# A transformer trunk on one Trainium2 core: turned blocks at fixed tiles, in source order

## The chip, the cores and the metric

The kernel runs on one core of a Trainium2 chip. The core has a matmul engine (TensorE, PE in the profile; its weight loads are PEld), three engines for elementwise work (VectorE or DVE, ScalarE or ACT, GpSimd or POOL), and SyncE (SP), which here only issues DMAs. Each engine works through its own queue of instructions in order; semaphores make one wait for another. The metric is the device time of one execution in microseconds, smaller is better.

## The reference

Two residual layers on 256 tokens of 2048 features, all in float32. Each layer is a token mixer and an MLP, each behind an RMSNorm:

```python
for i in range(DEPTH):                     # DEPTH = 2
    h = rms_norm(x, norm_mix[i])
    x = x + mixer(h, ...)                  # i = 0: stick-breaking attention; i = 1: indexer-selected softmax attention
    h = rms_norm(x, norm_mlp[i])
    x = x + jnp.square(jax.nn.relu(h @ w_up[i])) @ w_down[i]      # d_ff = 8192
```

Mixer A (layer 0) projects to q, k, v (16 heads of 128), weights each earlier token by sigmoid(z) times the product of (1 - sigmoid(z)) of the tokens between, and projects back. Mixer B (layer 1) scores tokens with a small indexer, keeps the best 64 per query, runs grouped softmax attention on them (16 query heads, 4 key heads), and projects back. Nearly all the arithmetic is in the weight matrices: the two MLPs alone have 4 x 2048 x 8192 weights.

## The kernel before, in words

**Weight tiles.** All dense products run as a list of 738 items (class `Item`), each one weight tile of 256 x 512 numbers (128 partitions x 1024). For item i the main loop at the end of `trunk` does, in this order: `split(i + 2)` (L762) makes of a raw weight tile a high part (ScalarE copy in a rounded format, through `copy`, L83) and a low part (VectorE subtraction, L774); `load(i + 7)` (L750) issues the DMA of a later raw tile on SyncE (L756; five raw buffers, so it waits for the split that frees one); the item's own matmuls (L271 to L273: three products, high x high, high x low, low x high, for two token halves and two blocks of 128 rows, twelve in all); then the item's `post` functions; then what is due. The split tiles have three buffers, so a split waits for the matmuls of the item three places earlier.

**Turned blocks.** Eight items (one group of 512 output columns) end in a 256 x 512 result with tokens on the partitions. Where the next product needs features on the partitions, `to_features` (L155) turns the block: VectorE transposes 32 x 32 squares into a tile `y` (L160), SyncE writes `y` to DRAM in four DMAs (`write`, L163 to L167, tile `td`), and reads it back turned (`read`, L169 to L171) into a tile `z`. A function `then` takes it up. `y` and `z` share the name `jx` and three buffers. There are 54 such blocks: 8 of q and k in mixer A, 2 of the indexer's queries in mixer B (these ten have no `then`), 12 of the residual stream x (`turn`, L180: four after each of mixer A, the first MLP, and mixer B), and 32 of the MLPs' hidden layers (`up_done`, L316). `turn` scales the block by a gain and splits it into the high and low parts of `xT`; `up_done` applies relu and square (L319) and splits into `hT` (copy L83, subtraction L322).

**When.** `later(n, f)` (L151) puts f into the list of the item n places on. Before the change a block that ends with item T is written with item T+2, read with T+5, and taken up in two halves with T+7 and T+8.

**Order.** These places are only the order in which the program is traced. The tile framework then schedules each engine's queue by its own model of time (`schedule_with_timeline_sim=True`), and may put an instruction ahead of earlier traced ones if its model says that it is ready sooner. `tc.keep_in_program_order(ins)` forbids that for one instruction: it can't be queued ahead of the one traced just before it on its engine. `pin` does the same for the first 16 items alone. So before the change the writes, the reads and the uptake were free to move, and so are the splits, loads and dense matmuls after item 16, before and after the change.

Groups run one after the other, except at the start of each section and in the output projections, where `side_by_side` (L292) interleaves two or three groups, so that they end close together. Mixer A's steps per pair of heads (`z_step`, `tail_step`, `o_step`) and mixer B's (`score_step` and the rest) hang on fixed items as `post` functions.

Of the kernel before, what the change touches and what calls it, by code (L numbers as in the profile page):

```python
# [9 lines left out]
F32 = mybir.dt.float32  # L10
F32R = mybir.dt.float32r
BF16 = mybir.dt.bfloat16
AF = mybir.ActivationFunctionType
OP = mybir.AluOpType
# [3 lines left out]
P = 128  # L18
# [41 lines left out]
def trunk(ctx, tc, x, x_t, gains_t, w_in_a, w_out_a, w_in_b, w_out_b, rel_bias, w_up, w_down, out):  # L60


    nc = tc.nc
# [10 lines left out]
    act, dve, pool, pe = nc.scalar, nc.vector, nc.gpsimd, nc.tensor  # L74

    pinned = [True]

    def pin(ins):
        if pinned[0]:
            tc.keep_in_program_order(ins)  # L80

    def copy(o, i, scale=1.0):
        pin(act.activation(o, i, AF.Copy, scale=scale))  # L83
# [67 lines left out]
    def later(n, f, *a):  # L151

        due[clock[0] + n].append(lambda: f(*a))

    def to_features(halves, place, then):  # L155


        y = tmp.tile([P, 8, P], F32, name="jx", bufs=3)
        for t, h in enumerate(halves):
            dve.transpose(y[:, 4 * t:4 * t + 4, :].rearrange("p k f -> p (k f)"), h)  # L160
        d = drp.tile([4, 32, 8, 4, 32], F32, name="td", bufs=4)

        def write():  # L163
            for a in range(4):
                nc.sync.dma_start(d[:, :, :, a, :].rearrange("b j n i -> j n b i"),  # L165
                                  y[32 * a:32 * a + 32].rearrange("p n (b i) -> p n b i", b=4))
            later(3, read)  # L167

        def read():  # L169
            z = place()  # L170
            nc.sync.dma_start(z, d.rearrange("b j n a i -> (b j) n (a i)"))  # L171
            if then is not None:
                later(2, then, z)

        later(2, write)

    def any_tile():
        return tmp.tile([P, 8, P], F32, name="jx", bufs=3)

    def turn(c, col):  # L180

        def half(z, js):
            for j in js:
                kt = 4 * c + j
                g = gains[:, col + kt:col + kt + 1]
                zk = z.rearrange("p (t k) q -> p t k q", t=2)[:, :, j, :]
                h, l = (xT[:, kt, i, :].rearrange("p (t q) -> p t q", t=2) for i in range(2))
                copy(h, zk, scale=g)
                dve.scalar_tensor_tensor(l, zk, g, h.bitcast(F32), op0=OP.mult, op1=OP.subtract)

        def split_in(z):
            half(z, (0, 1))
            later(1, half, z, (2, 3))

        to_features([xs[:, t, c * 512:(c + 1) * 512] for t in range(2)], any_tile, split_in)
        for t in range(2):
            square(c, t)

# [34 lines left out]
    def tokens_out(items, key, w, r0, c0, lhs, q, done, apart=False):  # L233


        def first(wh, wl):

            acc = accp.tile([P, 2, 512], F32, name="acc")
            accs[key] = [acc[:, t, :] for t in range(2)]
            L = lhs()  # L240
            for j in range(KB):
                for n, (part, wx) in enumerate(((0, wh), (1, wh), (0, wl))):
                    for t in range(2):
                        pin(pe.matmul(accs[key][t], L[:, j, part, t * P:(t + 1) * P], wx[:, j, :],
                                      start=(j == 0 and n == 0), stop=False))

        def last(acc, L, wh, wl):

            for t, c0, c1 in ((0, 0, 512), (1, 0, 256), (1, 256, 512)):
                for j in range(KB):  # L250
                    k = KB * q + j
                    for n, (part, wx) in enumerate(((0, wh), (0, wl), (1, wh))):
                        tc.keep_in_program_order(pe.matmul(
                            acc[t][:, c0:c1], L[:, k, part, t * P:(t + 1) * P], wx[:, j, c0:c1],
                            start=False, stop=(j, n) == (KB - 1, 2), skip_group_check=c0 > 0))

        def mm(wh, wl):
            if q == 0 and apart:
                accs[key] = [auxp.tile([P, 512], F32, name="aux") for _ in range(2)]
            elif q == 0:  # L260
                acc = accp.tile([P, 2, 512], F32, name="acc")
                accs[key] = [acc[:, t, :] for t in range(2)]
            acc, L = accs[key], lhs()
            if apart and q == QB - 1:
                last(acc, L, wh, wl)
                return
            for t in range(2):
                for j in range(KB):
                    k = KB * q + j
                    ts = slice(t * P, (t + 1) * P)  # L270
                    pin(pe.matmul(acc[t], L[:, k, 0, ts], wh[:, j, :], start=(k == 0), stop=False))  # L271
                    pin(pe.matmul(acc[t], L[:, k, 0, ts], wl[:, j, :], start=False, stop=False))  # L272
                    pin(pe.matmul(acc[t], L[:, k, 1, ts], wh[:, j, :], start=False,  # L273
                                  stop=(k == KT - 1)))
        it = Item(rows(w, r0 + KB * P * q, KB * P, c0, 512), KB, 512,
                  mm if len(items) >= LEAD else first, True)
        if q == QB - 1:
            it.post.append(lambda: done(accs.pop(key)))
        items.append(it)
# [24 lines left out]
    def mlp(l, next_col):  # L304
        items = []
        sec = {}
# [7 lines left out]
            dve.tensor_mul(sec["rs2"], rs, rs)  # L314

        def up_done(f, c, acc):  # L316
            def half(z, t):
                r = z[:, 4 * t:4 * t + 4]
                dve.scalar_tensor_tensor(r, r, 0.0, r, op0=OP.max, op1=OP.mult)  # L319
                h, l = (sec[f][:, 4 * c:4 * c + 4, i, t * P:(t + 1) * P] for i in range(2))  # L320
                copy(h, r)
                dve.tensor_sub(l, r, h.bitcast(F32))  # L322

            def split_in(z):
                if c == 0:
                    sec[f] = sec["pool"].tile([P, KT, 2, S], F32R, name="hT", bufs=2)
                half(z, 0)
                later(1, half, z, 1)

            to_features(acc, any_tile, split_in)  # L330

        def down_done(f, g, acc):
            if f < 3 or next_col is not None:
# [31 lines left out]
    def mixer_a():  # L365
# [102 lines left out]
            items[at].post.append(lambda n=n: square(n // 2, n % 2))  # L468
        items[2 * QB - 2].post.insert(0, stats)
        out_proj(items, w_out_a, lambda: st["oT"], 32, 2)  # L470
        for f, at in ((z_step, (23, 27, 47, 51, 71, 75, 87, 89)),
                      (tail_step, (27, 31, 51, 55, 75, 79, 92, 94)),
                      (o_step, (31, 34, 55, 58, 89, 91, 96, 98))):
            for hp, i in enumerate(at):
                items[i].post.append(lambda f=f, hp=hp: f(hp))
        return items, begin
# [6 lines left out]
    def bias_rows(pl):  # L483

        rb = pl.tile([P, 32], F32, name="rb", bufs=1)
        tc.keep_in_program_order(nc.scalar.dma_start(
            rb, rel_bias.unsqueeze(1).to_broadcast([HEADS, P // HEADS, 32])))
        bv = pl.tile([P, REL], F32, name="bv", bufs=1)  # L490
        for k, (lo, hi) in enumerate(zip(BUCKET_FROM, BUCKET_FROM[1:] + [256])):
            pool.tensor_copy(bv[:, 256 - hi:256 - lo], rb[:, k:k + 1].to_broadcast([P, hi - lo]))
            lo, hi = max(lo, 1), min(hi, 128)
            if lo < hi:
                pool.tensor_copy(bv[:, 255 + lo:255 + hi],
                                 rb[:, 16 + k:17 + k].to_broadcast([P, hi - lo]))
        bias["rows"] = bv

    def bias_spread(n):
        to = bv_d.rearrange("h (r q) d -> (h r) q d", r=P // HEADS)[:, 4 * n:4 * n + 4, :]  # L500
        tc.keep_in_program_order(
            nc.scalar.dma_start(to, bias["rows"].unsqueeze(1).to_broadcast([P, 4, REL])))

    def mixer_b():
# [61 lines left out]
        def score_step(m):  # L566
# [3 lines left out]
            ps = accp.tile([P, 2, 512], F32, name="acc")  # L570
            for t, cs, w in ((0, TOKS[0], P), (1, TOKS[1], S)):
                for i, lo in enumerate(halves):
                    tc.keep_in_program_order(
                        pe.matmul(ps[:, i, cs], st["qiT"][lo, m // 4, 4 * t + m % 4], kiT[lo, 0:w],
                                  start=True, stop=True))
            rl = mk([P, 2, 384], "rl")
# [31 lines left out]

        def bias_mask(n, h):
            b = st["bias", n][:, h:h + 2]  # L610
            tc.keep_in_program_order(
                dve.tensor_tensor(b, b, st["mask"].unsqueeze(1).to_broadcast([P, 2, 384]), op=OP.add))

        def normed(acc, key):
# [101 lines left out]
        def at(i, f, *a):  # L716
            items[i].post.append(lambda: f(*a))

        at(k0 + 1, wi_step)
        for m, d in enumerate((5, 5, 7, 7, 9, 9, 11, 11)):  # L720
            at(k0 + d, score_step, m)
        at(k0 + 9, lambda: turned("k", st["kT"], gains[:, 65:66]))
        at(k0 + 12, admit)
        for r in range(TOPK // 8):
            at(k0 + 13 + r // 2, top_step)
        at(k0 + 17, mask_step)
        for n in range(4):
            j = q0 + QB * n
            at(j, bias_load, n)
# [10 lines left out]
    n = 0  # L740
# [96 lines left out]
```

## Time and profile before

| | us |
|---|---|
| device time, median of 3 runs | 2160.94 (2158.61 to 2162.93) |
| the profiled execution | 2164.39 |
| span in its profile, first to last instruction | 2162.7 |

| engine | busy us | share |
|---|---|---|
| TensorE | 2105.7 | 97% |
| VectorE | 1236.8 | 57% |
| ScalarE | 969.6 | 45% |
| GpSimd | 28.5 | 1% |

The profile has several views. The *page* gives the busy time of each engine; matmuls are pipelined and their ends modelled, so that a matmul counts for longer than the distance to the next. The *waits* say which engine sat idle before which line, and what ended the wait: total us, times, longest. The *timeline* lists instructions by start and duration, with idle time and its cause in brackets. *Windows* give the busy time of a stretch, the clock granted to TensorE (1.00 is full) and the DMA engines' busy share. A *tile's* view gives the instructions that touch one tile, with the shortest, median and longest duration in ns, and its DMAs' times from issue to landing. Line numbers are those of the code above; L83 is the helper `copy`, so the tile's name tells which copy it is.

### The profile page before, as it was taken

The page shows a single profiled execution, that of the slowest core. Times are in us where ns is not written, and L with a number is a line of the kernel's source. Part 1 is how long each engine was busy: PE and PEld are TensorE (multiplying, and loading weights), DVE is VectorE, ACT ScalarE, POOL GpSimd, SP SyncE. Part 2 cuts the span into 40 slices and gives each one's busy share as a digit, 9 for nine tenths or more (in the row PEclk, how much of TensorE's full clock was granted, in tenths as well). Part 3 has the DMA queues.
Part 4 walks back from the last instruction along what each step waited for, and adds up shares of the span by engine and source line. Part 5 has one row for each costly group of instructions (what it writes and reads, how often), then busy time and mean ns, then how long its engine had stood idle before and what let it go on. Part 6 is the DMA issues. An engine that isn't in the chain of part 4 may idle for free.

```text
span 2162.7 us, 24794 instructions
## 1 busy us (share of the span) xinstructions
PE 2105.7 (97%) x9312; PEld 1726.7 (80%) x9312; DVE 1236.8 (57%) x1403; ACT 969.6 (45%) x1207; POOL 28.5 (1%) x71
## 2 busy tenths in 40 slices
PE   9999999999999999999999999999999999998999
PEld 7888887777788778778878788878777887887887
DVE  6555556565554644554565877665554555555554
ACT  6554555444333433433444566554443343344333
POOL 0200000000000000000000000000000000000000
PEclk9999999999999999999999999999999999999999
DMA  8788747788766866776688565598786687687664
GB/s 297 221 235 245 216 160 218 229 243 242 211 198 196 230 191 194 225 206 193 203 240 259 164 181 165 149 256 230 223 231 192 194 229 217 196 220 208 198 204 153
DMA packets 447113, 457.50 MB, mean 212 GB/s; under 512 B 240336, under 2 KB 250640, under 8 KB 446992
## 3 DMA queue, kind: packets, MB, share of 16 engines
q1 hardware_dynamic: 439136, 448.46, 70.9%
q10 hardware_dynamic: 7856, 7.45, 1.1%
q8 instruction: 73, 1.20, 0.2%
q14 instruction: 48, 0.39, 0.1%
HBM read 422.23 MB, written 33.55 MB: 211 GB/s over the span
## 4 chain that ended last, share of the span: by engine, by line
PE 73%; DMA 15%; DVE 5%; SPq 4%; issue 2%; ACT 1%; DVEq 0%; ACTq 0%
PE acc L272 23%; PE acc L273 23%; PE acc L271 22%; DMA jx<-td 6%; DMA td<-jx 6%; DVE w L774 3%; SPq L165 2%; SPq L756 2%; DMA wraw<-in_w_down_dram 2%; ACT w L83 1%; DVE jx L160 1%; DMA wraw<-in_w_up_dram 1%; DVE jx L319 1%; PE aux L660 0%; ACT xT L83 0%
## 5 line engine op out<-in xcount | busy, mean ns | idle before, releaser
L774 DVE TENSOR_TENSOR w<-wraw,w 128x1024 fp32r<-128x1024 f32 (+1 forms) x739 | 897.7, 1219 | 661.8 <-ACT w L83 659.7
L83 ACT ACTIVATE w<-wraw 128x1024 fp32r<-128x1024 f32 (+1 forms) x739 | 779.0, 1060 | 925.5 <-PE acc L273 896.0
L272 PE MATMUL acc<-w,xT 128*128 128x512 f32 x1632 | 641.9, 393 | 24.6 <-DVE w L774 24.6
L271 PE MATMUL acc<-w,xT 128*128 128x512 f32 x1632 | 639.6, 392 | 1.1 <-ACT w L83 0.7
L273 PE MATMUL acc<-w,xT 128*128 128x512 f32 x1632 | 638.3, 391 | 0.0
L272 PE MATMUL acc<-w,hT 128*128 128x512 f32 x992 | 390.2, 393 | 19.7 <-DVE w L774 19.7
L271 PE MATMUL acc<-w,hT 128*128 128x512 f32 x992 | 389.4, 393 | 0.2 <-ACT w L83 0.2
L273 PE MATMUL acc<-w,hT 128*128 128x512 f32 x992 | 389.2, 392 | 0.0
L272 PEld LDWEIGHTS acc<-w,xT 128*128 128x128 f32 x1632 | 307.2, 188 | 96.3 <-DVE w L774 33.7
L271 PEld LDWEIGHTS acc<-w,xT 128*128 128x128 f32 x1632 | 307.3, 188 | 66.8 <-ACT w L83 2.0
L273 PEld LDWEIGHTS acc<-w,xT 128*128 128x128 f32 x1632 | 307.3, 188 | 63.4 <-issue 0.3
L272 PEld LDWEIGHTS acc<-w,hT 128*128 128x128 f32 x992 | 188.1, 190 | 62.2 <-DVE w L774 22.9
L271 PEld LDWEIGHTS acc<-w,hT 128*128 128x128 f32 x992 | 188.0, 190 | 40.2 <-ACT w L83 0.9
L273 PEld LDWEIGHTS acc<-w,hT 128*128 128x128 f32 x992 | 188.3, 190 | 39.0
L319 DVE SCALAR_TENSOR_TENSOR jx<-jx 128x512 f32<-128x512 f32 x64 | 41.4, 689 | 144.4 <-DMA jx<-td 126.8
L272 PE MATMUL acc<-w,oT 128*128 128x512 f32 x256 | 101.1, 395 | 1.4 <-DVE w L774 1.4
L271 PE MATMUL acc<-w,oT 128*128 128x512 f32 x256 | 100.6, 394 | 0.8 <-ACT w L83 0.8
L273 PE MATMUL acc<-w,oT 128*128 128x512 f32 x256 | 100.3, 392 | 0.0
L83 ACT ACTIVATE hT<-jx 128x512 fp32r<-128x512 f32 x64 | 39.5, 631 | 125.0 <-DVE jx L319 125.0
L272 PEld LDWEIGHTS acc<-w,oT 128*128 128x128 f32 x256 | 48.1, 188 | 11.9 <-DVE w L774 2.1
L271 PEld LDWEIGHTS acc<-w,oT 128*128 128x128 f32 x256 | 48.0, 188 | 10.9 <-ACT w L83 1.2
L273 PEld LDWEIGHTS acc<-w,oT 128*128 128x128 f32 x256 | 48.1, 188 | 10.1 <-DVE oT L696 0.4
(143 smaller groups left out, 819.5 us busy)
## 6 DMA issues: line engine op xcount, KB each, us to landing
wraw<-in_w_up_dram SPq DMA_DIRECT2D x256, 512.0 KB, 4.6
wraw<-in_w_down_dram SPq DMA_DIRECT2D x256, 512.0 KB, 4.8
wraw<-in_w_in_a_dram SPq DMA_DIRECT2D x95, 512.0 KB, 4.7
wraw<-in_w_in_b_dram SPq DMA_DIRECT2D x64, 512.0 KB, 4.4
td<-jx SPq DMA_DIRECT2D x216, 128.0 KB, 4.7
jx<-td SPq DMA_DIRECT2D x44, 512.0 KB, 5.6
wraw<-in_w_out_a_dram SPq DMA_DIRECT2D x32, 512.0 KB, 3.7
wraw<-in_w_out_b_dram SPq DMA_DIRECT2D x32, 512.0 KB, 4.0
```

The lines of the kernel that those rows point to most:

```text
L83: pin(act.activation(o, i, AF.Copy, scale=scale))
L160: dve.transpose(y[:, 4 * t:4 * t + 4, :].rearrange("p k f -> p (k f)"), h)
L165: nc.sync.dma_start(d[:, :, :, a, :].rearrange("b j n i -> j n b i"), y[32 * a:32 * a + 32].rearrange("p n (b i) -> p n b i", b=4))
L271: pin(pe.matmul(acc[t], L[:, k, 0, ts], wh[:, j, :], start=(k == 0), stop=False))
L272: pin(pe.matmul(acc[t], L[:, k, 0, ts], wl[:, j, :], start=False, stop=False))
L273: pin(pe.matmul(acc[t], L[:, k, 1, ts], wh[:, j, :], start=False, stop=(k == KT - 1)))
L319: dve.scalar_tensor_tensor(r, r, 0.0, r, op0=OP.max, op1=OP.mult)
L756: pin(nc.sync.dma_start(raws[i][:, a], it.src[:, a]))
L774: pin(dve.tensor_sub(wl[:, a], raw[:, a], wh[:, a].bitcast(F32)))
```

## The change

The write, the read and the uptake of turned blocks are pinned to source order, other places are given to them, and the uptake is one operation to a tile instead of two halves:

- `write` at T+1 instead of T+2, and `read` four items later instead of three, so at T+5 as before; all five DMAs of a block are kept in program order on SyncE.
- `then` four items after the read instead of two, at T+9.
- `turn`: with T+9 four ScalarE copies, with T+10 four VectorE subtractions (before: two of each, in turn, at T+7 and at T+8).
- `up_done`: with T+9 one relu-square over the whole 128 x 1024 block, with T+10 one copy, with T+11 one subtraction (before: all three on each half, at T+7 and at T+8).
- Mixer A's and mixer B's steps that hang on turned data move by one or two items.

```diff
         def write():
             for a in range(4):
-                nc.sync.dma_start(...)
-            later(3, read)
+                keep(nc.sync.dma_start(...))
+            later(4, read)
 
         def read():
             z = place()
-            nc.sync.dma_start(z, d.rearrange("b j n a i -> (b j) n (a i)"))
+            keep(nc.sync.dma_start(z, d.rearrange("b j n a i -> (b j) n (a i)")))
             if then is not None:
-                later(2, then, z)
-
-        later(2, write)
+                later(4, then, z)
+
+        later(1, write)
...
-        def half(z, js):
-            for j in js:
-                kt = 4 * c + j
-                ...
-                copy(h, zk, scale=g)
-                dve.scalar_tensor_tensor(l, zk, g, h.bitcast(F32), op0=OP.mult, op1=OP.subtract)
-
-        def split_in(z):
-            half(z, (0, 1))
-            later(1, half, z, (2, 3))
+        def high(z):
+            for j, g, h, l in views():
+                keep(act.activation(h, z.rearrange("p (t k) q -> p t k q", t=2)[:, :, j, :],
+                                    AF.Copy, scale=g))
+            later(1, low, z)
+
+        def low(z):
+            for j, g, h, l in views():
+                keep(dve.scalar_tensor_tensor(l, ..., g, h.bitcast(F32), op0=OP.mult, op1=OP.subtract))
...
         def up_done(f, c, acc):
-            def half(z, t):
-                r = z[:, 4 * t:4 * t + 4]
-                dve.scalar_tensor_tensor(r, r, 0.0, r, op0=OP.max, op1=OP.mult)
-                ...
-                copy(h, r)
-                dve.tensor_sub(l, r, h.bitcast(F32))
+            def relu2(z):
+                ...
+                keep(dve.scalar_tensor_tensor(z, z, 0.0, z, op0=OP.max, op1=OP.mult))
+                later(1, high, z)
+
+            def high(z):
+                r, h, l = parts(z)
+                keep(act.activation(h, r, AF.Copy))
+                later(1, low, z)
+
+            def low(z):
+                r, h, l = parts(z)
+                keep(dve.tensor_sub(l, r, h.bitcast(F32)))
...
-        for f, at in ((z_step, (23, 27, 47, 51, 71, 75, 87, 89)),
-                      (tail_step, (27, 31, 51, 55, 75, 79, 92, 94)),
-                      (o_step, (31, 34, 55, 58, 89, 91, 96, 98))):
+        for f, at in ((z_step, (25, 28, 49, 52, 73, 76, 89, 91)),
+                      (tail_step, (29, 33, 53, 57, 77, 80, 93, 95)),
+                      (o_step, (33, 36, 57, 60, 89, 91, 97, 99))):
...
-        for m, d in enumerate((5, 5, 7, 7, 9, 9, 11, 11)):
+        for m, d in enumerate((6, 6, 8, 8, 10, 10, 12, 12)):
             at(k0 + d, score_step, m)
```

In mixer B, `admit`, the eight `top_step`s and `mask_step` follow one item later as well. Elsewhere `tc.keep_in_program_order` is only renamed to `keep`.

More of the change, by code (lines that the diff above doesn't have):

```diff
@@ L76, in trunk @@
     pinned = [True]
+    keep = tc.keep_in_program_order
     def pin(ins):
         if pinned[0]:
-            tc.keep_in_program_order(ins)
+            keep(ins)
     def copy(o, i, scale=1.0):
@@ L164, in write @@
             for a in range(4):
-                nc.sync.dma_start(d[:, :, :, a, :].rearrange("b j n i -> j n b i"),
-                                  y[32 * a:32 * a + 32].rearrange("p n (b i) -> p n b i", b=4))
-            later(3, read)
+                keep(nc.sync.dma_start(d[:, :, :, a, :].rearrange("b j n i -> j n b i"),
+                                       y[32 * a:32 * a + 32].rearrange("p n (b i) -> p n b i", b=4)))
+            later(4, read)
         def read():
             z = place()
-            nc.sync.dma_start(z, d.rearrange("b j n a i -> (b j) n (a i)"))
+            keep(nc.sync.dma_start(z, d.rearrange("b j n a i -> (b j) n (a i)")))
             if then is not None:
-                later(2, then, z)
-        later(2, write)
+                later(4, then, z)
+        later(1, write)
     def any_tile():
@@ L180, in turn, with views @@
     def turn(c, col):
-        def half(z, js):
-            for j in js:
+        def views():
+            for j in range(4):
                 kt = 4 * c + j
-                g = gains[:, col + kt:col + kt + 1]
-                zk = z.rearrange("p (t k) q -> p t k q", t=2)[:, :, j, :]
                 h, l = (xT[:, kt, i, :].rearrange("p (t q) -> p t q", t=2) for i in range(2))
-                copy(h, zk, scale=g)
-                dve.scalar_tensor_tensor(l, zk, g, h.bitcast(F32), op0=OP.mult, op1=OP.subtract)
-        def split_in(z):
-            half(z, (0, 1))
-            later(1, half, z, (2, 3))
-        to_features([xs[:, t, c * 512:(c + 1) * 512] for t in range(2)], any_tile, split_in)
+                yield j, gains[:, col + kt:col + kt + 1], h, l
+        def high(z):
[5 more added lines that the diff above has]
+            for j, g, h, l in views():
+                keep(dve.scalar_tensor_tensor(
+                    l, z.rearrange("p (t k) q -> p t k q", t=2)[:, :, j, :], g, h.bitcast(F32),
+                    op0=OP.mult, op1=OP.subtract))
+        to_features([xs[:, t, c * 512:(c + 1) * 512] for t in range(2)], any_tile, high)
         for t in range(2):
@@ L252, in last @@
                     for n, (part, wx) in enumerate(((0, wh), (0, wl), (1, wh))):
-                        tc.keep_in_program_order(pe.matmul(
+                        keep(pe.matmul(
                             acc[t][:, c0:c1], L[:, k, part, t * P:(t + 1) * P], wx[:, j, c0:c1],
@@ L316, in up_done, with parts @@
         def up_done(f, c, acc):
-            def half(z, t):
-                r = z[:, 4 * t:4 * t + 4]
-                dve.scalar_tensor_tensor(r, r, 0.0, r, op0=OP.max, op1=OP.mult)
-                h, l = (sec[f][:, 4 * c:4 * c + 4, i, t * P:(t + 1) * P] for i in range(2))
-                copy(h, r)
-                dve.tensor_sub(l, r, h.bitcast(F32))
-            def split_in(z):
+            def parts(z):
+                hT = sec[f][:, 4 * c:4 * c + 4].rearrange("p k i (t q) -> p i t k q", t=2)
+                return z.rearrange("p (t k) q -> p t k q", t=2), hT[:, 0], hT[:, 1]
+            def relu2(z):
                 if c == 0:
                     sec[f] = sec["pool"].tile([P, KT, 2, S], F32R, name="hT", bufs=2)
-                half(z, 0)
-                later(1, half, z, 1)
-            to_features(acc, any_tile, split_in)
+                keep(dve.scalar_tensor_tensor(z, z, 0.0, z, op0=OP.max, op1=OP.mult))
[7 more added lines that the diff above has]
+                keep(dve.tensor_sub(l, r, h.bitcast(F32)))
+            to_features(acc, any_tile, relu2)
         def down_done(f, g, acc):
@@ L487, in bias_rows @@
         rb = pl.tile([P, 32], F32, name="rb", bufs=1)
-        tc.keep_in_program_order(nc.scalar.dma_start(
+        keep(nc.scalar.dma_start(
             rb, rel_bias.unsqueeze(1).to_broadcast([HEADS, P // HEADS, 32])))
@@ L500, in bias_spread @@
         to = bv_d.rearrange("h (r q) d -> (h r) q d", r=P // HEADS)[:, 4 * n:4 * n + 4, :]
-        tc.keep_in_program_order(
+        keep(
             nc.scalar.dma_start(to, bias["rows"].unsqueeze(1).to_broadcast([P, 4, REL])))
@@ L572, in score_step @@
                 for i, lo in enumerate(halves):
-                    tc.keep_in_program_order(
+                    keep(
                         pe.matmul(ps[:, i, cs], st["qiT"][lo, m // 4, 4 * t + m % 4], kiT[lo, 0:w],
@@ L610, in bias_mask @@
             b = st["bias", n][:, h:h + 2]
-            tc.keep_in_program_order(
+            keep(
                 dve.tensor_tensor(b, b, st["mask"].unsqueeze(1).to_broadcast([P, 2, 384]), op=OP.add))
@@ L719, in mixer_b @@
         at(k0 + 1, wi_step)
-        for m, d in enumerate((5, 5, 7, 7, 9, 9, 11, 11)):
+        for m, d in enumerate((6, 6, 8, 8, 10, 10, 12, 12)):
             at(k0 + d, score_step, m)
         at(k0 + 9, lambda: turned("k", st["kT"], gains[:, 65:66]))
-        at(k0 + 12, admit)
+        at(k0 + 13, admit)
         for r in range(TOPK // 8):
-            at(k0 + 13 + r // 2, top_step)
-        at(k0 + 17, mask_step)
+            at(k0 + 14 + r // 2, top_step)
+        at(k0 + 18, mask_step)
         for n in range(4):
```

## The prediction, made before the changed kernel was run

> **What bounds the kernel now.** I read the page first, then the waits of TensorE, cut by stage, then the timeline of one stall on each engine, and last the rows that price the moved operations.
>
> ```profile
> span 2162.7 us, 24794 instructions
> PE 2105.7 (97%) x9312; PEld 1726.7 (80%) x9312; DVE 1236.8 (57%) x1403; ACT 969.6 (45%) x1207; POOL 28.5 (1%) x71
> ```
> TensorE is busy for 97% of the span, and no other engine comes near. So a gain must come out of the 57.0 us in which TensorE is idle (2162.7 - 2105.7), or out of its pace. The next rows are its waits between 340 and 1130 us (mixer A's output projection, first MLP, start of mixer B), then those from 1400 us to the end (mixer B's output projection, second MLP).
>
> ```profile
> PE acc L272 <- DVE w L774: 25.3, 16, 4.7
> PE acc L244 <- ACT w L83: 1.5, 2, 0.8
> PE acc L271 <- ACT w L83: 1.3, 3, 0.8
> ```
> ```profile
> PE acc L272 <- DVE w L774: 20.4, 14, 3.5
> PE acc L244 <- ACT w L83: 1.5, 1, 1.5
> PE acc L271 <- ACT w L83: 0.5, 1, 0.5
> ```
> The columns are total us, times and longest. That is 28.1 + 22.4 = 50.5 us in 37 waits, all for a weight tile not yet split: 45.7 us of it for the low half (VectorE, L774). What keeps VectorE and ScalarE from splitting in time stands in the waits of all engines:
>
> ```profile
>   DVE jx L319: 126.8, 27
>   ACT xT L83: 44.6, 13
> ```
> These are the waits on the turned blocks' tile jx, 40 of them (total us, times). Taken up are 32 up blocks and 12 residual blocks, 44 in all, so nearly each makes its engine wait. One case, on VectorE (start, us, what; idle before and its cause in brackets):
>
> ```profile
> 547.38 1.31 DVE L160 STREAM_TRANSPOSE jx<-acc 128x512 f32<-128x512 f32 x2 [0.40 <-PE acc L273]
> 548.61 1.18 DVE L774 TENSOR_TENSOR w<-wraw,w 128x1024 fp32r<-128x1024 f32 x1
> ...
> 556.63 1.23 DVE L774 TENSOR_TENSOR w<-wraw,w 128x1024 fp32r<-128x1024 f32 x1 [1.49 <-ACT w L83]
> 563.16 1.30 DVE L319 SCALAR_TENSOR_TENSOR jx<-jx 128x512 f32<-128x512 f32 x2 [5.30 <-DMA jx<-td]
> 564.37 1.22 DVE L774 TENSOR_TENSOR w<-wraw,w 128x1024 fp32r<-128x1024 f32 x1
> ```
> on ScalarE and SyncE:
> ```profile
> 555.53 1.06 ACT L83 ACTIVATE w<-wraw 128x1024 fp32r<-128x1024 f32 x1 [1.66 <-PE acc L273]
> 558.25 1.06 ACT L83 ACTIVATE w<-wraw 128x1024 fp32r<-128x1024 f32 x1 [1.66 <-PE acc L273]
> ```
> ```profile
> 557.34 0.34 SPq L171 DMA_DIRECT2D jx<-td  x1
> ```
> and on TensorE:
> ```profile
> 565.64 0.50 PE L272 MATMUL acc<-w,xT 128*128 128x512 f32 x1 [1.76 <-DVE w L774]
> ```
> Let T be the tile whose end frees the transposes at 547.38. One tile takes 558.25 - 555.53 = 2.72 us, so the subtractions at 548.61 and 556.63 belong to the steps T+1 and T+4. The relu (L319) stands right behind the latter, both halves of it, although the source asks for them at T+2+3+2 = T+7 and at T+8: the scheduler put them forward. The read was issued at 557.34 and had not landed, so VectorE stood for 5.30 us with the next weight's subtraction, whose high half was ready since 559.31, behind it. TensorE stopped for that. It is a queueing fault, not a lack of any engine's time.
>
> The clock adds to it. First three windows (span, PE busy with count, then the other engines, granted clock, DMA share, GB/s), then matmuls after a stall, then the mean clock.
>
> ```profile
> 200.00:300.00 100.00, 100.00 (x462) 83.47 (x461) 58.02 (x56) 56.22 (x63) 9.89 (x16) 1.00 0.72 209
> 600.00:700.00 100.00, 100.00 (x443) 82.82 (x442) 48.25 (x44) 38.34 (x36) 0.00 (x0) 1.00 0.67 200
> 700.00:780.00 80.00, 71.50 (x307) 58.13 (x306) 45.40 (x49) 32.27 (x35) 0.00 (x0) 0.98 0.74 208
> ```
> ```profile
> 590.26 0.51 PE L272 MATMUL acc<-w,hT 128*128 128x512 f32 x1 [2.56 <-DVE w L774]
> 591.00 0.63 PE L271 MATMUL acc<-w,hT 128*128 128x512 f32 x1
> 591.42 0.63 PE L272 MATMUL acc<-w,hT 128*128 128x512 f32 x1
> ```
> ```profile
> die 0 (median of its cores): 2162.7 us, clock 0.994
> ```
> Undisturbed, a matmul starts every 100/443 = 226 ns; after the stall at 590 us they start every 0.42 us. The first window also shows that mixer A's own blocks (q and k), whose data no early instruction waits for, turn beside a TensorE that never idles. So it is not the transfers as such that cost time.
>
> **What the change does, part by part.** First what goes. The 37 waits: 50.5 us. A wait hides more than it shows, because the modelled busy time of a matmul outlasts its pace:
>
> ```profile
> L272 PE MATMUL acc<-w,hT 128*128 128x512 f32 x992 | 390.2, 393 | 19.7 <-DVE w L774 19.7
> ```
> so each adds 393 - 226 = 167 ns, 37 times, 6.2 us. The clock: a mean of 0.994 leaves 0.006 x 2162.7 = 13.0 us; some of that time TensorE stood idle anyway and some is the kernel's end, so I take 11 us. Sum 50.5 + 6.2 + 11 = 67.7 us. A check by pace: 307 matmuls at 226 ns are 69.4 us, so the 80 us of the third window lose 10.6 us, and idle time (8.5), the hidden part of three stalls (0.5) and the clock (0.02 x 80 = 1.6) make 10.6 as well.
>
> The Trainium skill, "TensorE: Matmul & The Clock Gate", Part 1, says that the clock falls after about 3.4 us of idleness. By that only stalls near the longest (4.7 and 3.5 us in the waits above) would cost clock; as an estimate from the page's half clock, two or three windows of 3.4 us at half the work, about 5 us, and the sum would be about 62. Here the trace disagrees: the half pace at 591 us follows an idle time of 2.56 us. I keep the trace's 11 us.
>
> Now what comes. The rows that price it (min/median/max ns for operations; the landing row is of all transfers from and to jx; then KB and median us to landing):
>
> ```profile
> L165 SPq DMA_DIRECT2D td<-jx x216: 575/658/3334, 51.0 to 1985.6; - x108
> L83 ACT ACTIVATE hT<-jx x64: 629/631/636, 448.3 to 1998.0; 128x512 fp32r<-128x512 f32 x64
> L319 DVE SCALAR_TENSOR_TENSOR jx<-jx x64: 682/689/695, 447.6 to 1997.3; 128x512 f32<-128x512 f32 x64
> L83 ACT ACTIVATE xT<-jx,gains x64: 491/494/512, 3.3 to 1452.4; 128x256 fp32r<-128x256 f32 x64
> L189 DVE SCALAR_TENSOR_TENSOR xT<-jx,gains,xT x48: 442/483/490, 360.0 to 1452.9; 128x256 fp32r<-128x256 f32 x48
> DMA to landing us min/median/max: 2.3/4.7/8.8
> ```
> ```profile
> jx<-td SPq DMA_DIRECT2D x44, 512.0 KB, 5.6
> wraw<-in_w_up_dram SPq DMA_DIRECT2D x256, 512.0 KB, 4.6
> ```
> *Write at T+1, read at T+5, in SyncE's order.* The four writes stand behind the load of step T+1, which follows the subtraction ending at 549.8. Five issues of 0.66 us end at 553.1, and the last write lands 4.7 us later, at 557.8 (with 8.8, at 561.9). The read stands behind the load of T+5, which follows the subtraction of T+5, ending without the stall at 556.63 + 1.23 + 2.72 = 560.6; so it goes out at about 561.2, as a rule after the writes have landed. It lands at 566.8 (5.6 us) or 570.0 (8.8).
>
> *Uptake at T+9.* The relu is tied behind the subtraction of T+9, which ends at 557.86 + 5 x 2.72 = 571.5. So 1.5 us are left even for the longest landing, 4.7 us for the usual one. The pin holds it back: it can't stand in the queue earlier. That is why I count all 44 places as mended.
>
> *One operation to a tile.* The cover is this: a weight's high half starts when a tile's matmuls end, takes 1.06, its low half 1.23, and TensorE needs them two tiles later, at 2 x 2.72 = 5.44. So 3.1 us of delay per tile cost nothing. The relu over the whole tile is bounded by one subtraction of the same 128x1024 shape, 1.23, and two halves, 1.38; I take 1.3. VectorE then has 1.23 + 1.3 = 2.5 in 2.72 us, at T+9 and again at T+11; ScalarE 1.06 + 1.06 to 1.26 at T+10. Of residual blocks, ScalarE has 1.06 + 4 x 0.494 = 3.0 and VectorE 1.23 + 4 x 0.483 = 3.2, over by 0.3 and 0.5 for one tile, inside the 3.1. Nothing.
>
> *Later data.* The last residual block of a section ends with the section, so its four columns are now whole after step 9 of the next, and the interleaved first groups need them from step 12: no wait. Hidden blocks are used a whole down group later. Mixer A's steps move one or two tiles in a stretch where TensorE never idles (the row of 200 to 300 us), and their results are needed from tile 108 at the earliest where the last now comes at 99: nothing. The score steps of mixer B likewise, by one tile; they could win or lose some tenths, and I take zero.
>
> What stays. Where mixer B's output projection ends three blocks within six tiles, weights were late themselves:
>
> ```profile
> ACT w L83 <- DMA wraw<-in_w_up_dram: 3.8, 3, 2.0
> ```
> I leave 3 us for that and 3 us for tiles on which several blocks meet. The gain is 67.7 - 6 = 62 us. The profiled execution took 2164.4 us (span 2162.7 and 1.7 around it), so it would take 2102; it lies 3.5 us above the median of the runs, 2160.9, so I predict **2099 us**.
>
> **Rivals.** *Part of the stalls stays.* At a tile where transposes (1.31), relu (1.3), a low half (1.3, bounded like the relu), a residual sum (two 128x512, taken as two relu halves, 1.38) and the split (1.23) meet, VectorE has 6.5 us against 2.72 + 3.1 = 5.8, and TensorE waits 0.7 us or more. If 20 of 44 blocks do so at 1 us, 20 us come back: 2119. Against it: the source spreads these steps over single tiles, and the blocks end eight tiles apart but for the interleaved ones.
>
> *It does not do what it says.* If the relu still met an unlanded read, the time stayed at 2161. That needs a landing over 571.5 + 3.1 - 561.2 = 13.4 us; the longest is 8.8.
>
> *Slower, by late weights.* Reads and four writes in a row now stand at fixed places before loads. A raw buffer freed at 557.86 is wanted again five copies after 555.53, at 569.1: 11.3 us, of which the landing takes 4.6 and 6.7 is spare. If the writes (2.63) and the read (0.34) lost their cover wholly, each block cost 2.97, 44 blocks 131 us, less the 62: 2230. It decides from 1.5 us per block, (62 + 4.3)/44. What speaks for it is the 3.8 us above, and a DMA share of 0.74 that will rise to 0.74 x 80/69.4 = 0.85. Against it:
>
> ```profile
> SPq L756 <- DVE w L774: 1302.2, 562, 8.2
> ```
> SyncE spends 1302 us waiting for a buffer to come free: it is early, not late.
>
> *Late weights in the small.* If a load waited not only for the issue of the four writes but for their data too, it would land 2.63 + 4.7 + 4.6 = 11.9 us after its buffer came free, against 11.3: 0.6 us per block, 26 us in all, and the time would be about 2125. That TensorE never idles from 200 to 300 us, where blocks are written and read too, speaks against it. The Trainium skill, "DMA: Bandwidth & Descriptors", section "Queues, rings and completion order", says that each DMA engine takes the descriptors of an issuing queue in ring order, which is this mechanism. No row here shows the order inside the DMA engines; by that rule alone the sum would be the 2125.
>
> **How the numbers follow.** A measurement of this kernel tells about 0.2% (4.3 us) from no change. The forecast gets 0.72 (its own range 2089 to 2110: all 67.7 us and a little pace gained, or 11 us less), part stays 0.12, late weights in the small 0.04, no effect 0.04, slower 0.07, more than counted 0.01. Faster: 0.72 + 0.12 + 0.04 + 0.01 = 0.89. The range goes from 2088 (2160.9 less 67.7 and some 5 us of small gaps) to 2128, which takes in most of the two middle cases, so that about 0.2 is left out.
>
> **What would show it.** TensorE's waits on L774 fall from 45.7 us to a few; VectorE no longer waits on jx<-td at all, nor does SyncE before the read; the granted clock goes from 0.994 to 1.00; the relu comes 9 tiles after its transposes. I am wrong if VectorE still waits for jx, if waits for wraw appear on ScalarE, or if TensorE's idle time stays over 30 us.

## The result, and the profile after

The changed kernel takes 2095.75 us (median of 4 runs, 2094.14 to 2096.70) against 2161.93 us for the kernel before (median of 4 runs, 2158.61 to 2173.16, three of them those shown above). The ratio is 0.9684, with a 95% interval of 0.9648 to 0.9720: 3.2% faster. The forecast was 2099 us in a range from 2088 to 2128.

The page after, its head and the head of its chain of waits (shares of the span by engine):

```profile
span 2092.4 us, 24696 instructions
PE 2083.3 (100%) x9312; PEld 1720.7 (82%) x9312; DVE 1237.1 (59%) x1339; ACT 967.1 (46%) x1175; POOL 25.9 (1%) x71
```
```profile
PE 98%; DMA 1%; SPq 1%; ACT 0%; DVE 0%; issue 0%; DVEq 0%
```

The chain that ended last runs through TensorE for 98% of the span. The number of matmuls is the same; the time in which TensorE is idle went from 57.0 to 9.1 us (2092.4 - 2083.3). TensorE's waits, all of them:

```profile
PE acc L251 <- ACT w L85: 3.9, 3, 2.3
PE acc L121 <- DVE ones L93: 1.1, 1, 1.1
```

The columns are total us, times and longest. Nothing is left of the 45.7 us of waits for a low half. Two of the three waits that remain for a high half belong to the first items; the third is 2.3 us near 1393 us and comes back below. The window that lost 10.6 us before now loses none; the last columns are again granted clock, DMA share and GB/s:

```profile
700.00:780.00 80.00, 80.00 (x355) 66.24 (x354) 48.22 (x44) 33.76 (x32) 0.00 (x0) 1.00 0.77 234
```

355 matmuls instead of 307 in the same 80 us, and the DMA engines carry it at a share of 0.77. The tile jx after (ns min/median/max, then first and last start), whom it made wait on a read, and the landing times of its DMAs:

```profile
L331 DVE SCALAR_TENSOR_TENSOR jx<-jx x32: 1183/1216/1221, 452.2 to 1938.5; 128x1024 f32<-128x1024 f32 x32
L336 ACT ACTIVATE hT<-jx x32: 1042/1048/1067, 453.4 to 1939.8; 128x1024 fp32r<-128x1024 f32 x32
```
```profile
  ACT xT L192: 5.3, 3
```
```profile
DMA to landing us min/median/max: 2.2/4.8/9.2
```

VectorE no longer waits for a read at all (before: 126.8 us in 27 waits); ScalarE does three times, 5.3 us in all (before: 12 times, 44.4 us). SyncE hardly waits before a read any more; its rows before and after:

```profile
SPq L171 <- DMA td<-jx: 75.5, 58, 2.8
```
```profile
SPq L173 <- DMA td<-jx: 0.2, 1, 0.2
```

One block in the timelines of VectorE and SyncE:

```profile
516.23 1.31 DVE L162 STREAM_TRANSPOSE jx<-acc 128x512 f32<-128x512 f32 x2 [0.40 <-DMA wraw<-in_w_up_dram]
...
537.99 1.31 DVE L162 STREAM_TRANSPOSE jx<-acc 128x512 f32<-128x512 f32 x2 [0.40 <-DMA wraw<-in_w_up_dram]
539.23 1.18 DVE L787 TENSOR_TENSOR w<-wraw,w 128x1024 fp32r<-128x1024 f32 x1
540.33 1.22 DVE L331 SCALAR_TENSOR_TENSOR jx<-jx 128x1024 f32<-128x1024 f32 x1
```
```profile
519.10 4.09 SPq L167 DMA_DIRECT2D td<-jx  x4
523.29 6.54 SPq L769 DMA_DIRECT2D wraw<-in_w_up_dram  x4
529.99 0.34 SPq L173 DMA_DIRECT2D jx<-td  x1
```

The block transposed at 516.23 is read at 529.99 and squared at 540.33, just after the next block's transposes and with no idle time in front: 24.1 us after its transposes began, behind the subtraction of step T+9 (539.23). Before, it stood behind that of T+4.

### The profile page after: what moved, and what is told of

The parts are those of the page before. It is cut to its first block, busy times and chain, and to the rows that moved or that the text cites. A ratio compares the mean times of both kernels' runs of the same rounds, so it can differ in the third digit from the quotient of the medians.

```text
span 2092.4 us, 24696 instructions
## 1 busy us (share of the span) xinstructions
PE 2083.3 (100%) x9312; PEld 1720.7 (82%) x9312; DVE 1237.1 (59%) x1339; ACT 967.1 (46%) x1175; POOL 25.9 (1%) x71
## 4 chain that ended last, share of the span: by engine, by line
PE 98%; DMA 1%; SPq 1%; ACT 0%; DVE 0%; issue 0%; DVEq 0%
PE acc L278 31%; PE acc L280 31%; PE acc L279 31%; PE acc L251 1%; PE aux L673 1%; SPq L167 0%; PE acc L411 0%; PE aux L457 0%; PE acc L587 0%; DMA jx<-td 0%; PE aux L279 0%; PE aux L280 0%; PE aux L278 0%; DMA wraw<-in_w_in_a_dram 0%; PE aux L690 0%; PE aux L651 0%
## 5 line engine op out<-in xcount | busy, mean ns | idle before, releaser
L279 PEld LDWEIGHTS acc<-w,hT 128*128 128x128 f32 x992 | 186.2, 188 | 38.7
L278 PEld LDWEIGHTS acc<-w,hT 128*128 128x128 f32 x992 | 186.2, 188 | 38.7
L280 PEld LDWEIGHTS acc<-w,hT 128*128 128x128 f32 x992 | 186.2, 188 | 38.6
L162 DVE STREAM_TRANSPOSE jx<-acc 128x512 f32<-128x512 f32 x68 | 44.7, 696 | 14.4 <-PE acc L280 11.2
L294 DVE SCALAR_TENSOR_TENSOR xs<-acc,rs,xs 128x512 f32<-128x512 f32 x56 | 39.5, 747 | 11.2 <-PE acc L280 11.2
```

Of the source, the lines that this page charges most:

```text
L294: dve.scalar_tensor_tensor(xc, acc[t], scale[:, t:t + 1], xc, op0=OP.mult, op1=OP.add)
```

## The experiments

Each run was timed against the kernel before on the same chip. The theory is *queue place*: the time hangs on where the uptake stands in VectorE's and ScalarE's queues against the read's landing. The rivals are *the transfers* (rival A: SyncE stood before reads, with loads behind it) and *the distances and the single operation* (rival B: the pins are idle). The kernel before takes 2160.2 to 2169.4 us (medians) on the chips used, so the runs are best compared by their ratios, or by times on one chip.

### No pin at all

```diff
-                keep(nc.sync.dma_start(d[:, :, :, a, :]...))     # write, read, and the five
+                nc.sync.dma_start(d[:, :, :, a, :]...)           # uptake operations alike
```

> The changed kernel with its new places and one operation to a tile, but with no pin on the turned blocks' writes, reads and uptake. Theory (queue place: what counts is where the uptake stands in VectorE's and ScalarE's queues against the read's landing): the schedule puts the relu behind the subtraction of T+4 again, as in the kernel before, so TensorE's stalls come back, 2145 to 2170 us. Rival A (the transfers: what counts is that SyncE no longer stands before a read, 75.5 us before): the DMAs are free, also 2145 to 2170. Rival B (the new distances and the single operation carry the gain, the pins are idle): 2095 us.

Measured 2150.58 us, ratio 0.9927 (0.9903 to 0.9950). The new distances and the single operation alone gain 0.7% of the 3.2. TensorE's waits and VectorE's timeline at a stall:

```profile
PE acc L279 <- DVE w L787: 39.8, 26, 4.1
```
```profile
578.49 1.23 DVE L787 TENSOR_TENSOR w<-wraw,w 128x1024 fp32r<-128x1024 f32 x1 [1.50 <-ACT w L85]
585.43 1.22 DVE L331 SCALAR_TENSOR_TENSOR jx<-jx 128x1024 f32<-128x1024 f32 x1 [5.72 <-DMA jx<-td]
```

The relu, traced at T+9, stands behind the subtraction of T+4 again and waits there 5.72 us. Rival B falls: a place in the source binds nothing that is free to move.

### Only the uptake free, only the DMAs free

```diff
 # uptake free: the five uptake operations lose their keep(...)
 # DMAs free:   the four writes and the read lose their keep(...)
```

> The changed kernel with the writes and reads pinned, the uptake free. Its relu is queued behind the subtraction of T+7. Queue place: by the steps of the changed kernel the read lands 13.8 + 6.4 = 20.2 us after the transposes begin, 1.6 us after that subtraction ends; the cover of 3.1 us takes that at the usual landing and not at the longest, so 2096 to 2112 us. Rival A: 2096. Rival B: 2095. A theory that needs every pin: about 2160.

> The changed kernel with the uptake pinned at T+9 to T+11, the writes and reads free. Queue place: the reads go out earlier than in the changed kernel, the uptake still comes after the landing, 2093 to 2099 us, SyncE waiting some 70 us before reads at no cost. Rival A: the gain is lost for the most part, 2140 to 2160.

With the uptake free 2103.31 us (ratio 0.9703, 0.9680 to 0.9727), with the DMAs free 2093.16 us (0.9659, 0.9638 to 0.9681). The first row is SyncE's with the DMAs free, the second VectorE's with the uptake free, the third TensorE's there:

```profile
SPq L173 <- DMA td<-jx: 76.8, 63, 3.2
```
```profile
DVE jx L331 <- DMA jx<-td: 44.9, 29, 3.1
```
```profile
PE acc L279 <- DVE w L787: 4.2, 8, 0.8
```

With the DMAs free SyncE waits before reads for as long as in the kernel before (there 75.5 us), and the kernel is as fast as the changed one: rival A is out. With the uptake free and the reads pinned late, the schedule itself put the relu behind T+7 (presumably since its model sees the late read); VectorE then waits 44.9 us for reads, 1.5 us at a time, and the 3.1 us of cover swallow most of it. So the pins on the DMAs alone gain most of what the change gains, 2103 against 2151 us without any pin, but by the same way: they move the relu to a later place in the queue. On the same chip they stay 10 us behind the pinned uptake (2103.31 against 2093.16).

### The kernel before, pinned at its old places

```diff
-                copy(h, zk, scale=g)
-                dve.scalar_tensor_tensor(l, zk, g, ...)
+                keep(act.activation(h, zk, AF.Copy, scale=g))
+                keep(dve.scalar_tensor_tensor(l, zk, g, ...))
 # likewise up_done's three; and for "everything", the four writes and the read
```

> The kernel before with its old places (write at T+2, read at T+5, halves at T+7 and T+8), everything of the turned blocks pinned to source order. Queue place: the first half of the relu stands behind the subtraction of T+7, the read goes out at T+5 as in the changed kernel, so the same as with the free uptake: 2096 to 2112 us. Rival B (the distances are needed): 2140 to 2160.

> The kernel before with one thing changed: the uptake (its halves at T+7 and T+8) is pinned to source order; the writes and reads stay free, at their old places. Queue place: the read goes out about 10 us after the transposes begin and lands at 15.6, the subtraction of T+7 ends at 18.6, so no wait: 2094 to 2104 us, nearly the whole gain. Rival (old places need the later uptake as well, as when everything was pinned at the old places): 2115 to 2125.

Everything pinned: 2121.44 us (0.9794, 0.9767 to 0.9821), 9 us above what I expected. Only the uptake pinned: 2093.95 us (0.9665, 0.9633 to 0.9696). VectorE, ScalarE and SyncE with everything pinned:

```profile
564.29 1.23 DVE L776 TENSOR_TENSOR w<-wraw,w 128x1024 fp32r<-128x1024 f32 x1 [1.50 <-ACT w L85]
569.79 0.69 DVE L321 SCALAR_TENSOR_TENSOR jx<-jx 128x512 f32<-128x512 f32 x1 [4.28 <-DMA jx<-td]
```
```profile
570.52 0.63 ACT L323 ACTIVATE hT<-jx 128x512 fp32r<-128x512 f32 x1 [3.55 <-DVE jx L321]
571.06 1.05 ACT L85 ACTIVATE w<-wraw 128x1024 fp32r<-128x1024 f32 x1
```
```profile
554.32 5.72 SPq L167 DMA_DIRECT2D td<-jx  x4
```
```profile
562.65 0.34 SPq L173 DMA_DIRECT2D jx<-td  x1
```

The writes take 5.72 us to issue where I had taken 2.63, the read goes out at 562.65, and the relu can start 7.1 us later, at 569.79. It has waited 4.28 us, more than the cover; and because relu and copy stand in the same step, ScalarE waits as well, with the next weight's high half behind it at 571.06. (Another 2.3 us of TensorE's waits in this run are for turned q and k, as in the last run below.) Leave the DMAs free, and the read goes out as soon as the writes have landed, some 9 us after the transposes begin (the rows below: transposes of this kernel at 538.73, read at 547.81), early enough for T+7:

```profile
538.73 1.31 DVE L162 STREAM_TRANSPOSE jx<-acc 128x512 f32<-128x512 f32 x2
```
```profile
547.81 0.34 SPq L173 DMA_DIRECT2D jx<-td  x1
```

So five pins on the kernel before, all on the uptake, give the whole gain. The later places are needed only because the change also holds the DMAs back.

### Halves instead of one operation

```diff
+                half(z, 0)                 # at T+9: relu, copy, subtraction of one half, all pinned
+                later(1, half, z, 1)       # at T+10: the other
```

> The changed kernel with the uptake in two halves as before (each half relu, copy and subtraction in one step), pinned, at T+9 and T+10. Queue place, with the cover of 3.1 us per tile: VectorE and ScalarE have a little more to do per tile, the copy waits for the relu of its own step and pushes the next weight's high half by about 0.9 us, inside the cover, so 2094 to 2100 us. Rival (one operation to a tile is a part of the gain): 2105 to 2120.

Measured 2094.52 us (0.9669, 0.9631 to 0.9706). One operation to a tile costs nothing and gains nothing that can be told here.

### Four raw weight buffers

```diff
-RAW = 5
+RAW = 4
```

> The changed kernel with four raw weight buffers instead of five, which takes 2.7 of the 6.7 us that a weight's load has to spare. If loads are early and the writes ahead of them hide (theory): 2096 to 2108 us. If loads stand behind the writes' data as well as their issue (late weights): 4.1 to 5.4 us of issue alone are more than the 4.0 us left, each block loses 1 us or more, 2130 to 2180.

Measured 2096.50 us (0.9678, 0.9646 to 0.9710), the same as with five. ScalarE's waits for weights do grow, from 9.8 us in 7 waits to 60.4 in 29; the largest row:

```profile
ACT w L85 <- DMA wraw<-in_w_in_a_dram: 17.9, 11, 4.1
```

but TensorE hardly sees them: its waits are 5.6 us in all, against 5.0 with five buffers. With 2.7 us less to spare, loads behind four writes are still in time, or late by no more than ScalarE can make up. Both rivals of late weights fall, except at one place.

### The place that is left: three blocks together

ScalarE in the changed kernel where mixer B's output projection ends, then the half-paced matmuls after it:

```profile
1378.31 1.06 ACT L85 ACTIVATE w<-wraw 128x1024 fp32r<-128x1024 f32 x1 [3.47 <-DMA wraw<-in_w_out_b_dram]
...
1385.99 1.06 ACT L85 ACTIVATE w<-wraw 128x1024 fp32r<-128x1024 f32 x1 [2.50 <-DMA wraw<-in_w_up_dram]
1390.07 1.70 ACT L192 ACTIVATE xT<-jx,gains 128x256 fp32r<-128x256 f32 x4 [3.01 <-DMA jx<-td]
```
```profile
1392.77 1.72 PE L251 MATMUL acc<-w,xT 128*128 128x512 f32 x4 [2.29 <-ACT w L85]
```

Three blocks end within six items; weights and reads both come late. Writing the third one four items later spreads them:

```diff
-        later(1, write)
+        later(wait, write)        # wait = 5 for group 2 of mixer B's output projection, else 1
```

> The changed kernel, and the third of the three blocks that end close together in mixer B's output projection is written five items after its end instead of one, with read and uptake after it. Theory: the one stall left behind the start, 2.3 us near 1393 us, and the half clock after it (3.4 us, 1.7 lost) come from late weights behind three blocks' transfers, so 2090 to 2093.5 us. Rival (that stall has another cause): 2094 to 2097.

> The changed kernel with the third block of mixer B's output projection written later (as in the spread run) and with writes and reads free instead of pinned. Queue place: the pins on the DMAs do not matter, so the same as the spread run, 2088 to 2091.5 us. Rival (the pins on the DMAs keep weights on time): 2093 or more.

> The changed kernel itself, unchanged, as the yardstick on the same chip: 2093 to 2098 us.

Spread, 2090.09 us (2089.37 to 2090.33; ratio 0.9646, 0.9619 to 0.9674); spread with free DMAs, 2093.85 (0.9691, 0.9675 to 0.9707); the changed kernel again beside the latter, 2094.41 (0.9693, 0.9677 to 0.9709). The same stretch of the changed kernel, of the changed kernel again, of the spread one and of the spread one with free DMAs:

```profile
1355.00:1400.00 45.00, 42.71 (x180) 34.29 (x179) 30.21 (x39) 25.54 (x43) 0.00 (x0) 0.96 0.86 235
```
```profile
1355.00:1400.00 45.00, 42.97 (x184) 33.62 (x182) 30.02 (x39) 26.58 (x45) 0.00 (x0) 1.00 0.87 234
```
```profile
1355.00:1400.00 45.00, 45.00 (x200) 37.28 (x199) 33.65 (x48) 26.95 (x44) 0.00 (x0) 1.00 0.88 238
```
```profile
1355.00:1400.00 45.00, 42.98 (x188) 34.60 (x187) 29.73 (x40) 25.35 (x40) 0.00 (x0) 1.00 0.84 226
```

The spread run lost the stall. It has 20 matmuls more in these 45 us than the first profile of the changed kernel, some 4.5 us, and 16 more than the second, some 3.6 us; the second has the stall too (1.8 us) but no half clock after it. The spread run is the fastest version here, though it ran on another chip than the yardstick, and the two ratios' intervals lie close (up to 0.9674, from 0.9677). What speaks for the order as well are the runs' own times, which do not overlap (2093.64 is the lowest of all nine runs of the changed kernel; the run in halves took 2094.52 on the spread run's own chip), and this window. With free DMAs a stall stays (1.4 us), and my expectation for that run was wrong: two of the third block's writes go out ahead of the second block's read again, so the spread is undone in part (SyncE of that run):

```profile
1376.13 2.46 SPq L167 DMA_DIRECT2D td<-jx  x2
1378.68 4.07 SPq L769 DMA_DIRECT2D wraw<-in_w_up_dram  x1
1382.84 0.42 SPq L173 DMA_DIRECT2D jx<-td  x1
```

That this order brings the stall back is read from the two traces, not tried by itself. It is the one use of the pins on the DMAs that the runs point to: they hold a place that was chosen.

### The mixers' steps at their old items

```diff
-        for f, at in ((z_step, (25, 28, 49, 52, 73, 76, 89, 91)),
+        for f, at in ((z_step, (23, 27, 47, 51, 71, 75, 87, 89)),   # and the others of both mixers
```

> The changed kernel with mixer A's z, tail and o steps and mixer B's score, admit, top and mask steps at their old items. The prediction counted their move as nothing: 2093 to 2098 us. Rival (they must follow the later reads, or TensorE waits for turned q and k): 2105 to 2125, with waits of TensorE on qk<-td.

Measured 2097.49 us (0.9707, 0.9691 to 0.9723), against 2094.41 for the changed kernel on the same chip. TensorE now does wait for a turned block:

```profile
PE acc L411 <- DMA qk<-td: 1.1, 1, 1.1
PE acc L411 <- PE acc L280: 0.7, 1, 0.7
```

That is 1.8 us, near 75 us. The rest of the 3 us lies elsewhere: this run's profile has one stretch of 3.4 us at half clock, at 1396 us behind the stall of the three blocks, and the yardstick's has none (mean clock 0.999 and 1.000). The steps' move was not a gain, but it kept the pinned, later reads from costing about 2 us.

## Why the prediction held, point by point

**What goes.** The waits went as predicted: 48.2 of the 50.5 us, all but the 2.3 us at 1393. The clock rose from 0.994 to 0.999. In the profile before there are seven stretches of 3.4 us at half clock ahead of the kernel's end, in the one after there is one. In such a stretch a matmul starts every 0.427 us instead of 0.227, and the eight that fit lose 1.6 us; six stretches make 9.6 us, where 11 were predicted. The hidden part of the waits is the term that was too small. One stall of the kernel before:

```profile
745.71 0.39 PE L271 MATMUL acc<-w,xT 128*128 128x512 f32 x1
748.59 0.50 PE L272 MATMUL acc<-w,xT 128*128 128x512 f32 x1 [2.50 <-DVE w L774]
748.93 0.40 PE L273 MATMUL acc<-w,xT 128*128 128x512 f32 x1
749.17 0.40 PE L271 MATMUL acc<-w,xT 128*128 128x512 f32 x1
```

From the first to the third start are 3.22 us, where two matmuls take 0.45 undisturbed: 2.77 us are lost, and the wait shows 2.50. The first matmul behind the wait takes 0.34 us to the next, and the ten after it together another 0.07 more than undisturbed. The prediction had counted only the part ahead of the wait, 0.167 us. In the stalls of the kernel before that stand alone and cost no clock, the loss beyond the wait shown is 0.29 to 0.34 us; as an estimate, 37 times 0.31 is 11.5 us instead of 6.2. The sum is then 48.2 + 9.6 + 11.5 = 69.3 of the 70.3 us by which the span fell.

**The clock rule.** The stall of 2.29 us near 1393 us halved the pace behind it; the stall of 2.50 us just shown cost no clock. What decides can be read from the traces. Leave out the first 20 us and the end of each run: then 17 stretches at half clock are left in the thirteen profiles, each 3.41 us long (two of them 6.83), and within a profile their starts lie whole multiples of 3.413 us apart. Cut the time into windows on this grid. In the window that ended where a stretch begins, TensorE had always been idle for 1.78 us or more, by the modelled ends of its matmuls; no window at full clock with 1.76 us or less was followed by one. Two stalls of the kernel before, two windows for each (idle is the span less PE busy; the last columns are clock, DMA share and GB/s):

```profile
587.21:590.62 3.41, 0.84 (x5) 0.38 (x4) 2.85 (x4) 2.12 (x4) 0.00 (x0) 1.00 0.20 79
590.62:594.04 3.42, 3.42 (x10) 2.64 (x9) 3.06 (x4) 1.01 (x2) 0.00 (x0) 0.50 0.51 175
744.22:747.63 3.41, 1.88 (x9) 1.22 (x7) 1.52 (x3) 0.79 (x2) 0.00 (x0) 1.00 0.65 228
747.63:751.05 3.42, 2.46 (x11) 2.00 (x12) 3.42 (x5) 2.35 (x3) 0.00 (x0) 1.00 0.41 104
```

The first stall, 2.56 us, lies in one window, and the next runs at half clock. The second is cut by the grid into 1.5 and 1.0 us, and nothing happens. So a stall between 1.8 and 3.4 us costs clock or not by where it falls. The Trainium skill ("TensorE: Matmul & The Clock Gate", Part 1) has the clock fall after an idle window of about 3.4 us, and the window run free of the kernel. The traces agree with the grid and not with the idle window: a little over half of one was enough. The prediction took its 11 us from the mean clock and did not hang on this rule.

**Write and read.** The mechanism was right and two sizes were off. Four writes in a row take 4.1 to 5.4 us to issue between 515 and 570 us, not 2.63, and the read lands 6.4 us after its issue (median), not 5.6:

```profile
jx<-td SPq DMA_DIRECT2D x44, 512.0 KB, 6.4
```

The read still went out 13.8 us after the transposes begin, as forecast (561.2 - 547.38), since the load ahead of it decides that. The margin before T+9 took the later landing.

**Uptake at T+9.** Right, to the step. But the prediction priced the change as one piece. The runs part it: the pin on the uptake alone gives the whole gain, and beside it the pins on the DMAs and the later places cancel each other. Without it the pins on the DMAs give most of the gain, since they too put the relu later in the queue. The prediction had given SyncE's 75.5 us before reads no price; the run with free DMAs shows that it has none.

**One operation to a tile.** Nothing, as predicted; the relu of 128x1024 takes 1.22 us and the copy 1.05, one subtraction's and one copy's worth, so the lower bounds were the right ones.

**Later data.** Nothing, as predicted; without the move it would have cost some 2 us.

**What stays.** I had left 3 us for the three blocks of mixer B and 3 us for tiles on which blocks meet. The first was 2.3 us of stall with 1.6 us of clock behind it, and ScalarE's waits for weights there grew from 3.8 to 6.0 us; the second did not come at all. That the forecast came within 3.3 us of the result is partly luck. In the profiled executions the span fell by 70.3 us, where 61.7 had been forecast: 3 of these 8.6 us are the second reserve, some 5 the hidden part of the waits. But the profiled execution before lay 3.5 us above the median of its runs and the one after 1.6 us below its own, which takes 5 us off the distance again.

**The rivals.** Part of the stalls staying shows only where the pins are taken away or the old places kept. Slower by late weights, and late weights in the small, fell with the four raw buffers: at least the 2.7 us that they took away had been to spare. The DMA share that I put at 0.85 is 0.77, at 234 GB/s instead of 208, so it did not grow with the bytes. No run here separates the order inside the DMA engines from the room that the loads have.

## What to carry to other kernels

When an in-order engine waits for a DMA and the bound engine's next input is queued behind that wait, compare the place in the queue with the place in the source: a scheduler that (presumably) takes transfers as landed too early moves the consumer forward, and later places in the source help little (0.7% here). Pin the consumer before touching the transfers; here five pins in the source gave 3% of the time. Then work out each step's slack against the longest landing seen, because a pinned consumer that comes up before the landing is a stall of its own (the uptake at T+7 took 2121 us with the DMAs held back, 2094 with them free).

## What the runs showed of the hardware

Issuing a DMA is not of fixed length. In the changed kernel one and the same write takes SyncE 569 ns at the least, 667 in the median and 4799 at the most, and four in a row took 4.09 us in the stretch shown above; in the spread run, where the blocks are close, 8.23. It is the third that is held. Past the first 60 us, the first, second and fourth write of a block take 0.58, 0.66 and 0.67 us in the median in the changed kernel, the third 2.2 (1.5 at the least). A load of weights that comes up behind two writes is held in the same way, although a load takes 0.37 us otherwise: the 80 such loads of the kernel before take 2.2 us in the median. SyncE in the run without any pin:

```profile
570.57 1.29 SPq L167 DMA_DIRECT2D td<-jx  x2
571.96 2.81 SPq L769 DMA_DIRECT2D wraw<-in_w_down_dram  x1
```

What holds it is not shown; the DMA engines' share is 0.87 both in the 4.09 us and in the 8.23 us. But it means that a chain of issues must be priced by rows of such a chain, not by the median of one.
